# Third score chunk of the first token tile: from the attention heads to behind the last output projection

## The chip, the cores and the metric

The kernel runs on one core of a Trainium2 chip. The metric is the device time of one execution in microseconds (us). TensorE is called PE below, VectorE DVE, ScalarE ACT, GpSimd POOL, and SyncE SP; SP issues most of the loads from device memory. Each engine executes its own instructions in a fixed order and waits on semaphores for what others make. A "slot" is one buffer of a pool of on-chip memory: a load into a slot can start only when the last reader of what the slot held before is done.

## What is computed

One decoder layer on 512 tokens with 1024 features. Its first half is attention by two groups of heads, whose outputs are concatenated and projected (`w_o`). Its second half finds, for every token and each of 8 retrieval heads, 16 of 16384 experts by two sets of 128 keys:

```python
qp = (h @ w_pq).reshape(b, s, PEER_HEADS, 2, PEER_HALF)          # 1024 -> 2048 query features
sc = einsum("bshpd,hpnd->bshpn", qp, sub_keys)                   # 128 scores for each of 16 key sets
s1, i1 = top_k(sc[..., 0, :], 16);  s2, i2 = top_k(sc[..., 1, :], 16)
cand = s1[..., :, None] + s2[..., None, :]                       # pairs, then the best 16 of them
top_s, top_c = top_k(cand, 16);  gate = softmax(top_s)
# out = sum over the chosen experts e of gate_e * v_e * gelu(u_e . h)
```

`w_pq` is handled in four chunks of 512 columns (2 MB each). A chunk c gives the scores of two retrieval heads, that is four sets of 128 scores for each token.

## The kernel before

The 512 tokens are four tiles of 128. Tile 0 is the "sparse" tile: the rows of its chosen experts are gathered from memory. Tiles 1 to 3 are the "dense" ones: every expert is computed for them, in 128 blocks, and multiplied by a matrix of gates.

The program text gives an order of steps; a scheduler then sorts each engine's instructions by its own model. The stages, with their place in the profile before:

- Until about 206 us the modulation (`w_ada` through a pool called `g8` of two slots of 8 KB per partition, loaded as 1 MB pieces), then the input projections, then the heads of attention, tile 0 first and then tiles 3, 2, 1, to about 357 us.
- Into the heads of tiles 3, 2 and 1 a second list of steps is woven, `first`: for tile 0 its output projection, its second norm (`hidden2`), and for chunks 0, 1 and 2 the projection to queries and scores (`queries_one`, called `q1(c)`) followed by `top(0, c)`, the 16 best of each of the four score sets on DVE. A `q1` is 32 matmuls, recorded as 64, on L173, a copy `qpT` on ACT (L681), four matmuls against the keys (L685) and a copy `sc` on ACT (L687). `top(i, c)` calls `best`: two rounds of "8 largest" and "their places" for each set (L731 to L735).
- From 357 to 391 us the output projection of tiles 3, 2 and 1 (L385 to L387, three products of split numbers for every one). Then `hidden2` of these tiles, a norm, eight PE transposes (L136), a scale and shift (L167 on ACT, L165 on DVE), and a split into `h2hi` (ACT, L724) and `h2lo` (DVE, L725). Chunk 3 of tile 0, `q1(3)`, stands here.
- From 411 to 490 us `queries(T, c)` for the dense tiles together, four chunks, each with split weights `whi` (a cast on ACT, L373) and `wlo` (a subtraction on DVE, L374), woven with `top` of the chunk before.
- From about 490 us the dense pass in two halves: u (block inputs `ut`, split into `uhi` on ACT, L871, and `ulo` on DVE, L872; matmuls L940 to L942) to about 1050 us, and v (L986) to the end at 1684.5 us. Beside the first blocks runs the list `work`: `pick(0)`, which joins tile 0's best and chooses 16 experts per head in two halves of four heads (`select`, L743 to L778), then the remaining `top` steps, `pick` and `gates` of the dense tiles. The gathers of tile 0 follow its `pick`.

Where weights lie decides when they can be loaded. `w_pq` for `q1` goes through the pool `ld` of four slots of 4 KB per partition, so a chunk fills all four; `w_o` and the split weights of `queries` (L371, in `halves`) pass through the same four slots. `wload` doubles the piece when the pool is `g8`, and ties such a load behind the last load issued before it, by `issue_after`. The pool `g8` is free between the modulation and the score buffers `sc` of `queries`.

Of the kernel before, what the change touches and what calls it, by code (L numbers as in the profile page):

```python
# [38 lines left out]
DENSE = [1, 2, 3]  # L39
# [23 lines left out]
def pipe(tasks, lag=1):  # L63

    live, tasks, n = [], iter(tasks), 0
    while True:
        t = next(tasks, None)
        if t is not None:
            live.append((n, t))
        elif not live:  # L70
            return
        for s, g in reversed(live):
            if (n - s) % lag == 0 and next(g, live) is live:
                live = [x for x in live if x[1] is not g]
        n += 1
        yield


class Layer:
# [275 lines left out]
            self.wt[name] = self.wload(self.I[name], alloc)  # L355
        return self.wt[name]

    def weights1(self, name, src):

        if (name, 1) not in self.wt:  # L360
            self.wt[name, 1] = self.wload(src, self.ld)
        return self.wt[name, 1]

    def halves(self, name, src, raw, new):
# [271 lines left out]

    def w_pq1(self, c):
        self.keys("keys1", c)
        return self.weights1(f"w_pq{c}", self.I["w_pq"][c])

    def keys(self, name, c):

# [362 lines left out]
    def build(self):  # L1005
# [13 lines left out]
        def run(g):  # L1019
            for _ in g:  # L1020
                pass

        def seq(*gs):
            for g in gs:
                yield from g

        def weave(main, fill, n, skip=0, every=1, rest=True):
            for m, _ in enumerate(main):
                if m >= skip and (m - skip) % every == 0:
                    for _ in range(n):  # L1030
                        next(fill, None)
            if rest:
                run(fill)

        def spread(g, n):
            for _ in g:
                for _ in range(n):
                    yield

        def top(i, c):  # L1040
            self.best(i, T[i], c)
            yield

        def prep(f, *a):
            f(*a)
            yield

        def idle(n):
            for _ in range(n):
                yield  # L1050
# [18 lines left out]
        for g in (m[0], h0, h1, m[1], m[0], m[2], m[1], m[3], m[2], m[3], h0, h1):  # L1069
# [4 lines left out]
        q1 = lambda c: self.queries_one(T[0], c)  # L1074
        first = seq(prep(self.w_o, 0, 0), idle(1), self.out_proj(0, T[0], 0), prep(self.w_o, 0, 1), idle(1),
                    self.out_proj(0, T[0], 1), prep(self.w_pq1, 0), idle(2), spread(self.hidden2(0, T[0]), 3), idle(3),
                    spread(q1(0), 2), prep(self.w_pq1, 1), top(0, 0), spread(q1(1), 2), prep(self.w_pq1, 2), top(0, 1),
                    spread(q1(2), 2), top(0, 2))
        tasks = hs[2:] + base + self.heads(0, T)
        skip = len(tasks) + 10  # L1080
        main = pipe(tasks + self.heads(3, T) + self.heads(2, T) + self.heads(1, T), 3)
# [6 lines left out]
        run(first)  # L1088
        o = [self.out_proj(i, T[i], half) for i, half in ((3, 0), (2, 0), (1, 0), (3, 1), (2, 1), (1, 1))]
        n = [self.hidden2(i, T[i]) for i in (3, 2, 1)]  # L1090
        run(pipe(o[:3] + [prep(self.w_pq, 0)] + o[3:5] + n[:1] + o[5:] + [prep(self.w_pq1, 3)] + n[1:] + [q1(3)], 2))
        for c in range(4):
            tops = [top(i, c - 1) for i in DENSE if 0 < c < 3] + ([top(0, 3)] if c == 1 else [])
            weave(self.queries(T, c), seq(*tops), 1)
        work = seq(pick(0), *(top(i, c) for c in (2, 3) for i in DENSE),
                   *(g for i in DENSE for g in (pick(i), gates(i))))
# [64 lines left out]
```

## Time and profile before

| what | value |
|---|---|
| median of 3 runs | 1683.05 us (1680.65 to 1687.23) |
| profiled execution | 1686.27 us |
| its span on the core | 1684.5 us |
| granted PE clock, mean | 0.979 |
| PE busy | 1586.5 us, 94% of the span |
| DVE busy | 1261.8 us, 75% |
| ACT busy | 679.3 us, 40% |
| DMA | 451.36 MB, 268 GB/s |

A share of the whole span says little about the change, since it touches three stretches: the heads (to 357 us), the passage from the output projection to the first query products (391 to 435 us), and the sorting that runs on DVE from 434 us into the first dense blocks. Each is read for itself: which engine is full there, and what the others wait for. In the list of windows a row holds the bounds of a stretch, its length, then for PE, PE's weight loads, DVE, ACT and POOL the busy time with the count of instructions, the granted PE clock (1.00 is 2.4 GHz, 0.50 is 1.2 GHz), the DMA share and GB/s.

### The profile page before, as it was taken

To read this page: it belongs to the slowest core of one execution; us is meant where nothing else is said; L and a number is where in the kernel's file an instruction comes from. 1 tells how busy PE (TensorE), PEld (TensorE's weight loads), DVE (VectorE), ACT (ScalarE), POOL (GpSimd) and SP (SyncE) were. 2 spreads that over 40 slices of the span, in tenths; PEclk is the share of its full clock that TensorE was granted. 3 is DMA by queue.
4 is the path that set the end of the run, shared out by engine and by line. 5 is a ranking of instruction groups with operands and counts; after the bars stand their busy time and mean duration, and the time that the engine had idled before them with its cause. 6 is when DMAs were issued, how large, how long until landed. Compare 5 with 4: busy or idle time off the path is not lost.

```text
span 1684.5 us, 25155 instructions
## 1 busy us (share of the span) xinstructions
PE 1586.5 (94%) x8993; PEld 1392.5 (83%) x8993; DVE 1261.8 (75%) x2626; ACT 679.3 (40%) x1072; POOL 483.4 (29%) x514
## 2 busy tenths in 40 slices
PE   5999999998978999999999999999999999999996
PEld 2977498987977998999999999887777777877885
DVE  2533363586799789999998996687887788887863
ACT  3521364454323434663564465333333333333331
POOL 1302510001012455336226422223332323333311
PEclk7899999998989999999999999999999999999998
DMA  7354613358144788998999899999999999999852
GB/s 289 130 184 161 221 39 119 126 192 287 53 154 142 225 279 266 316 353 302 315 346 336 285 344 352 370 366 355 356 364 345 359 352 360 366 377 375 276 184 100
DMA packets 200913, 451.36 MB, mean 268 GB/s; under 512 B 17874, under 2 KB 103890, under 8 KB 198740
## 3 DMA queue, kind: packets, MB, share of 16 engines
q1 hardware_dynamic: 103252, 277.18, 46.4%
q0 software_dynamic: 38656, 139.48, 23.4%
q10 hardware_dynamic: 58880, 33.11, 6.5%
q8 instruction: 70, 1.15, 0.3%
q14 instruction: 55, 0.45, 0.1%
HBM read 393.07 MB, written 56.63 MB: 267 GB/s over the span
## 4 chain that ended last, share of the span: by engine, by line
PE 77%; DVE 10%; DMA 5%; ACT 3%; issue 2%; POOL 0%; SPq 0%; POOLq 0%; ACTq 0%; DVEq 0%
PE acc L986 30%; PE bank L942 7%; PE bank L941 7%; PE bank L940 7%; PE bank L386 4%; PE bank L387 4%; PE bank L173 4%; PE bank L385 4%; DVE ulo L872 3%; PE bank L820 2%; PE bank L136 2%; DMA G<-gst 2%; PE bank L564 2%; PE bank L579 2%; DMA ut<-in_peer_uT 1%
## 5 line engine op out<-in xcount | busy, mean ns | idle before, releaser
L986 PE MATMUL acc<-vhi,whl 128*128 128x512 f32 x1536 | 422.3, 393 | 22.7 <-ACT vhi L871 22.7
L986 PEld LDWEIGHTS acc<-vhi,whl 128*128 128x128 f32 x1536 | 287.3, 188 | 91.4 <-ACT vhi L871 29.2
L942 PE MATMUL bank<-hhi,ulo 128*128 128x384 f32 x1024 | 347.1, 339 | 15.4 <-DVE ulo L872 15.3
L940 PE MATMUL bank<-hhi,uhi 128*128 128x384 f32 x1024 | 345.5, 338 | 12.5 <-ACT uhi L871 12.4
L941 PE MATMUL bank<-hlo,uhi 128*128 128x384 f32 x1024 | 347.9, 340 | 0.0
L831 POOL DMA_INDIRECT gat<-in_peer_v,ids x128 | 155.6, 1216 | 325.7 <-DVE y L859 304.9
L871 ACT CAST uhi<-ut 128x1024 fp32r<-128x1024 f32 x128 | 134.4, 1050 | 275.5 <-PE bank L941 222.8
L831 POOL DMA_INDIRECT gat<-in_peer_u,ids x128 | 142.9, 1116 | 342.7 <-DVE sact L849 326.2
L986 PE MATMUL acc<-vlo,whl 128*128 128x512 f32 x768 | 239.2, 392 | 0.0
L872 DVE TENSOR_TENSOR ulo<-ut,uhi 128x1024 fp32r<-128x1024 f32 x128 | 170.7, 1334 | 58.1 <-ACT uhi L871 57.7
L942 PEld LDWEIGHTS bank<-hhi,ulo 128*128 128x128 f32 x1024 | 194.2, 190 | 21.1 <-DVE ulo L872 20.5
L940 PEld LDWEIGHTS bank<-hhi,uhi 128*128 128x128 f32 x1024 | 194.1, 190 | 14.6 <-ACT uhi L871 14.1
L941 PEld LDWEIGHTS bank<-hlo,uhi 128*128 128x128 f32 x1024 | 194.1, 190 | 0.5
L872 DVE TENSOR_TENSOR vlo<-vt,vhi 128x1024 fp32r<-128x1024 f32 x128 | 156.5, 1222 | 48.1 <-ACT vhi L871 46.4
L976 ACT CAST whl<-ge 128x384 fp32r<-128x384 f32 x128 | 65.4, 513 | 297.1 <-PE acc L986 279.6
L849 DVE CUSTOM_DVE_ANT_0 scr<-gat,h2r 128x1024 bf16<-128x1024 f32 x128 | 170.8, 1334 | 0.0
L986 PEld LDWEIGHTS acc<-vlo,whl 128*128 128x128 f32 x768 | 144.4, 188 | 31.9
L859 DVE SCALAR_TENSOR_TENSOR y<-gat,swgt,y 128x1024 f32<-128x1024 f32 x127 | 170.7, 1344 | 0.1
L871 ACT CAST vhi<-vt 128x1024 fp32r<-128x1024 f32 x128 | 133.7, 1048 | 79.5 <-PE acc L986 59.4
L977 DVE TENSOR_TENSOR whl<-ge,whl 128x384 fp32r<-128x384 f32 x128 | 71.0, 556 | 65.1 <-ACT whl L976 58.0
L822 ACT ACTIVATE gst<-bank 128x512 f32<-128x512 f32 x96 | 96.9, 1120 | 6.3 <-DMA G<-gst 6.3
L772 POOL TENSOR_TENSOR prod<-hit,cid 128x800 f32<-128x800 f16 x32 | 70.6, 2207 | 20.6 <-DVE hit L769 18.4
(252 smaller groups left out, 2231.6 us busy)
## 6 DMA issues: line engine op xcount, KB each, us to landing
ut<-in_peer_uT SPq DMA_DIRECT2D x128, 512.0 KB
vt<-in_peer_v SPq DMA_DIRECT2D x128, 512.0 KB
G<-gst ACTq DMA_DIRECT2D x24, 1024.0 KB
gt<-G SPq DMA_DIRECT2D x96, 256.0 KB
ged<-ge SPq DMA_DIRECT2D x120, 192.0 KB
ge<-ged SPq DMA_DIRECT2D x120, 192.0 KB
w<-in_w_ada SPq DMA_DIRECT2D x16, 1024.0 KB
w<-in_w_pq SPq DMA_DIRECT2D x32, 512.0 KB
```

The costliest lines, as they stand in the source:

```text
L772: g.tensor_tensor(out=prod, in0=hit, in1=cid[:, r][:, None, :, None].to_broadcast(shape), op=OP.mult)
L822: nc.scalar.activation(st[:, :, q + t4:q + t4 + 4].rearrange("p i t -> p t i"), pb.rearrange("p (t i) -> p t i", t=4), AF.Copy, scale=1.0 ...
L831: self.nc.gpsimd.indirect_dma_start(out=t, out_offset=None, in_=self.I[table], in_offset=bass.IndirectOffsetOnAxis(ap=ids[:, k:k + 1], axi ...
L849: v.tensor_tensor_reduce(out=scr, in0=u, in1=self.rows, op0=OP.mult, op1=OP.add, scale=1.0, scalar=0.0, accum_out=a[:, k:k + 1])
L859: v.scalar_tensor_tensor(out=self.y, in0=t, scalar=w[:, k:k + 1], in1=self.y, op0=OP.mult, op1=OP.add)
L871: nc.scalar.copy(hi, src)
L872: self.last_split = eng.tensor_tensor(out=lo, in0=src, in1=hi, op=OP.subtract)
L940: pe.matmul(A, uh[:, k, :], hh, start=(k == 0), stop=False)
L941: pe.matmul(A, uh[:, k, :], hl, start=False, stop=False)
L942: pe.matmul(A, ul[:, k, :], hh, start=False, stop=(k == KD - 1))
L977: nc.vector.tensor_tensor(out=wl, in0=w, in1=wh, op=OP.subtract)
L986: self.nc.tensor.matmul(self.acc[t][half], w[:, ts], v[:, half * 512:(half + 1) * 512], start=(b == n == 0), stop=(b == NK - 1 and n == 2))
```

## The change

`q1(2)` and `top(0, 2)` leave the list `first`. The weights of chunk 2 go into the two slots of `g8`, as two loads of 1 MB, and `q1(2)` stands behind the last output projection, ahead of `q1(3)`. Of the two steps that now sort after the heads, `top(0, 2)` is woven into the second chunk of `queries` and `top(0, 3)` into the third; before, `top(0, 3)` was in the second.

```diff
-    def weights1(self, name, src):
+    def weights1(self, name, src, alloc=None):
         if (name, 1) not in self.wt:
-            self.wt[name, 1] = self.wload(src, self.ld)
+            self.wt[name, 1] = self.wload(src, alloc or self.ld)
...
-        return self.weights1(f"w_pq{c}", self.I["w_pq"][c])
+        return self.weights1(f"w_pq{c}", self.I["w_pq"][c], self.g8 if c == 2 else self.ld)
...
-                    spread(q1(0), 2), prep(self.w_pq1, 1), top(0, 0), spread(q1(1), 2), prep(self.w_pq1, 2), top(0, 1),
-                    spread(q1(2), 2), top(0, 2))
+                    spread(q1(0), 2), prep(self.w_pq1, 1), top(0, 0), spread(q1(1), 2), top(0, 1))
...
-        run(pipe(o[:3] + [prep(self.w_pq, 0)] + o[3:5] + n[:1] + o[5:] + [prep(self.w_pq1, 3)] + n[1:] + [q1(3)], 2))
+        run(pipe(o[:3] + [prep(self.w_pq, 0)] + o[3:5] + n[:1] + o[5:]
+                 + [prep(self.w_pq1, 2), prep(self.w_pq1, 3)] + n[1:] + [q1(2), q1(3)], 2))
...
-            tops = [top(i, c - 1) for i in DENSE if 0 < c < 3] + ([top(0, 3)] if c == 1 else [])
+            tops = [top(i, c - 1) for i in DENSE if 0 < c < 3] + ([top(0, c + 1)] if c in (1, 2) else [])
```

On PE, behind the output projection, the transposes of tiles 2 and 1 (`xn`) and the projections of tile 0 (`x_2352`, its second-norm output) stand in this order, as a difference between the two programs:

```order
 L136 MATMUL bank<-ident,xn 128x128 x8
 L173 MATMUL bank<-x_2352,w 128x128 x32
-L136 MATMUL bank<-ident,xn 128x128 x16
-L685 MATMUL bank<-keys,qpT 128x128 x4
+L136 MATMUL bank<-ident,xn 128x128 x8
+L173 MATMUL bank<-x_2352,w 128x128 x32
+L136 MATMUL bank<-ident,xn 128x128 x8
+L685 MATMUL bank<-keys,qpT 128x128 x8
 L385 MATMUL bank<-h2hi,whi 128x384 x4
```

`q1(2)` takes the place that `q1(3)` had, and `q1(3)` stands between the transposes of tile 2 and those of tile 1, whose result every first product of the dense queries needs.

On ACT, from the copy of the queries of tile 0's last chunk on, before (`x_3405` is tile 2, `x_3435` tile 1, `whi` the split weights of the dense queries' chunk 1, `x` the scaled norm):

```order
L681 COPY qpT<-bank 128x512
L373 CAST whi<-w 128x1024
L167 ACTIVATE x_3405<-bank,b_119,a_118 128x128
L373 CAST whi<-w 128x1024
L167 ACTIVATE x_3405<-bank,b_119,a_118 128x128
L373 CAST whi<-w 128x1024
L167 ACTIVATE x_3435<-bank,b_119,a_118 128x128
L167 ACTIVATE x_3405<-bank,b_119,a_118 128x128
L724 CAST h2hi<-x_3405 128x2x128
```

and now (`x_3359` is tile 1; tile 2 is done ahead of this copy):

```order
L681 COPY qpT<-bank 128x512
L167 ACTIVATE x_3359<-bank,b_119,a_118 128x128 x2
L373 CAST whi<-w 128x1024
L167 ACTIVATE x_3359<-bank,b_119,a_118 128x128
L724 CAST h2hi<-x_3359 128x2x128
L687 COPY sc<-bank 128x512
L167 ACTIVATE x_3359<-bank,b_119,a_118 128x128
L724 CAST h2hi<-x_3359 128x2x128
L687 COPY sc<-bank 128x512
L373 CAST whi<-w 128x1024
```

One cast of chunk 1's weights still stands ahead of tile 1's first `h2hi`, and three stood ahead of tile 2's before; the two score copies of tile 0 stand between tile 1's `h2hi` casts.

On SP, the loads of weights, as a difference (L291 is `q1`'s, L371 that of split weights; 128x2048 is a piece in `g8`):

```order
 L371 DMA w<-in_w_pq 128x1024 x3
 L371 DMA w<-in_w_o 128x1024 x4
+L291 DMA w<-in_w_pq 128x2048 x2
 L291 DMA w<-in_w_pq 128x1024 x4
 L371 DMA w<-in_w_pq 128x1024 x12
```

Chunk 2's two pieces stand directly ahead of chunk 3's four; earlier in the list, four pieces of 0.5 MB for chunk 2 are gone.

On DVE the 16 instructions of "8 largest" and places that belong to `top(0, 2)`, with the four replacements between the rounds, leave the heads. The last steps of `select` for tile 0's first half now stand between the first `wlo` subtractions of `w_o`. By the order, the sorting instructions of `top(0, 2)` fall ahead of the ninth to thirteenth `ulo`; from the thirteenth `ulo` on, as many sorting instructions have passed as before.

## Rows read from the trace of the kernel before

**Rows 1.** Windows view: bounds, length, busy us (count) by engine, clock, DMA share, GB/s:

```profile
327.70:356.90 29.20, 28.67 (x255) 28.01 (x253) 27.43 (x169) 15.64 (x45) 2.87 (x12) 1.00 0.30 103
...
391.20:410.80 19.60, 12.79 (x98) 12.14 (x96) 12.86 (x24) 13.80 (x29) 4.45 (x8) 0.88 0.88 300
410.80:434.60 23.80, 23.61 (x129) 23.10 (x130) 12.55 (x34) 10.53 (x18) 0.00 (x0) 0.89 0.74 232
434.60:496.40 61.80, 56.62 (x353) 56.42 (x351) 59.43 (x378) 14.60 (x28) 7.22 (x21) 0.99 0.15 47
```

**Rows 2.** Chain that ended last, heads of attention: start us, us, what:

```profile
316.12 7.15 PE bank L173 x64
...
344.69 0.78 DVE tv L731 x4
...
357.13 1.14 DVE wlo L374
```

**Rows 3.** Timeline of PE: start us, us, line, operation, [idle before <-releaser]:

```profile
332.10 7.31 PE L173 MATMUL bank<-x,w 128*128 128x128 f32 x64
...
341.92 1.06 PE L685 MATMUL bank<-keys,qpT 128*128 128x128 f32 x8
...
392.10 7.31 PE L173 MATMUL bank<-x,w 128*128 128x128 f32 x64
401.49 1.09 PE L136 MATMUL bank<-ident,xn 128*128 128x128 f32 x8 [2.08 <-DVE xn L347]
...
404.72 1.69 PE L685 MATMUL bank<-keys,qpT 128*128 128x128 f32 x8
410.76 1.65 PE L385 MATMUL bank<-h2hi,whi 128*128 128x384 f32 x4 [4.35 <-ACT h2hi L724]
```

**Rows 4.** Timeline of DVE: a chunk of sorting, in the heads and later:

```profile
344.61 0.87 DVE L731 MAX8 tv<-sc 128x8 f32<-128x128 f32 x4
345.39 0.07 DVE L732 MATCH_VALUE_LOAD ti<-tv,sc 128x8 f32 x1
...
345.66 0.07 DVE L733 MATCH_VALUE_LOAD sc<-tv,sc 128x8 f32 x1
...
345.91 0.41 DVE L566 CUSTOM_DVE_ANT_0 s<-bank,mask 128x256 f32<-128x256 f32 x1
...
440.93 0.09 DVE L733 MATCH_VALUE_LOAD sc<-tv,sc 128x8 f32 x1
...
442.04 0.09 DVE L733 MATCH_VALUE_LOAD sc<-tv,sc 128x8 f32 x1
```

**Rows 5.** Timeline of SP's DMA issues of score weights:

```profile
375.42 7.39 SPq L291 DMA_DIRECT2D w<-in_w_pq  x4
398.10 32.84 SPq L371 DMA_DIRECT2D w<-in_w_pq  x12
```

**Rows 6.** Windows view, around the start of the dense queries (columns as before):

```profile
360.00:380.00 20.00, 19.96 (x89) 16.16 (x88) 14.76 (x17) 7.85 (x8) 0.00 (x0) 1.00 0.89 308
...
404.00:406.00 2.00, 2.00 (x12) 2.00 (x11) 2.00 (x3) 1.85 (x4) 0.62 (x2) 0.50 1.05 420
...
410.00:416.00 6.00, 5.05 (x15) 4.54 (x16) 6.00 (x26) 3.48 (x9) 0.00 (x0) 0.50 1.05 380
```

**Rows 7.** Timeline of ACT: first weight cast for the second query chunk:

```profile
402.73 1.05 ACT L373 CAST whi<-w 128x1024 fp32r<-128x1024 f32 x1 [1.51 <-DMA w<-in_w_pq]
```

**Rows 8.** Timeline of PE, queries at full clock:

```profile
418.89 0.33 PE L385 MATMUL bank<-h2hi,whi 128*128 128x384 f32 x1
419.06 0.33 PE L386 MATMUL bank<-h2lo,whi 128*128 128x384 f32 x1
```

**Rows 9.** Windows view, first blocks of the dense pass:

```profile
550.00:560.00 10.00, 9.06 (x53) 8.74 (x52) 6.63 (x29) 5.80 (x7) 6.59 (x7) 1.00 0.92 315
560.00:570.00 10.00, 10.00 (x59) 10.00 (x58) 6.75 (x8) 4.04 (x6) 5.24 (x3) 1.00 0.78 266
```

**Rows 10.** PE's waits, 440 to 1060 us: total, times, longest:

```profile
PE bank L942 <- DVE ulo L872: 15.3, 13, 3.4
```

## The prediction, made before the changed kernel ran

> **What bounds the kernel now.** I read the list of windows first, one row for each stretch that the change touches, then the chain of work that ended last, then the timelines of PE, DVE, ACT and SP inside these stretches. In the last 29.2 us of the heads PE is busy for 28.67 us and DVE for 27.43 [rows 1]: the two are nearly full together, ACT with 15.64 us is not. The chain runs there through DVE, from the end of one projection on PE to the first `wlo` of the output projection at 357.13 us [rows 2], so DVE's order of softmax pieces and sorting sets the end of the heads, and PE's fill is close behind it. Between the last output and the queries, 391.2 to 410.8 us, nothing is full: PE works 12.79 of 19.6 us [rows 1], and its timeline has two holes, one until 401.49 us, where the transposes wait for a norm, and one of 4.35 us until 410.76 us, where the first product waits for `h2hi` from ACT [rows 3]. From 410.8 to 434.6 us PE is full (23.61 of 23.8) and DVE half idle; from 434.6 to 496.4 us DVE is full (59.43 of 61.8) [rows 1]. Work that leaves the heads therefore leaves a full stretch, and its PE part goes to a loose one, its DVE part to one that is as full as the one it left.
>
> **The heads: less of both engines.** On PE `q1(2)` is one block of 7.31 us and four key products, 1.06 us recorded for eight interleaved records, about half of it new time [rows 3]: 7.31 + 0.53 = 7.8 us go, and 28.67 - 7.8 = 20.9 us stay. On DVE the price of a chunk of sorting is read from start to next start, because the recorded times overlap: the four first "8 largest" take 345.39 - 344.61 = 0.78 us, a first search with its load 345.66 - 345.39 = 0.27, a replacement with its load 345.91 - 345.66 = 0.25 [rows 4]. With 0.2 for a single "8 largest", the chunk is 0.78 + 4 x 0.27 + 4 x (0.25 + 0.2 + 0.27) = 4.7 us. About 1.3 us of the last `select` steps leave as well (eight short instructions of 0.1 to 0.2 us, estimated from the same rows). DVE keeps 27.43 - 4.7 - 1.3 = 21.4 us. If DVE's idle time in the stretch (29.2 - 27.43 = 1.8) stays, the stretch takes 23.2 us, 6.0 less. With no idle time it is 21.4, 7.8 less. At the other end, a heads stage that waits on its own softmax chain, from scores to DVE to ACT to PE, keeps half of it: 3.0 less. I take **-6.0**, nearest to the engine that the chain names.
>
> **The output projection.** The `select` steps of 1.3 us now stand between the first four `wlo`. PE's first products there wait for these. Some of the steps fall before the first product anyway, so I take **+0.3**, from 0 to +1.3.
>
> **From the last output to the queries.** `q1(2)` fits where `q1(3)` was, 392.10 to 399.4 us (times of before, without the shift). Tile 2's transposes keep 401.49 to 402.4 us, since their norm is not earlier. `q1(3)` then takes 7.31 us at full clock, to 409.8; but the granted clock was 0.50 (1.2 GHz) at 404 to 406 us, after the hole in PE's work before 401.49 [rows 3, 6], and if the block runs so until 406 us, 1.8 us are added: 409.8 to 411.6, I take 410.7. Only as it ends are the four `ld` slots free, so the loads of the dense queries' chunk 1 are issued at about 410.7 instead of 398.10 [rows 5]. Their first cast had its data 402.73 - 398.10 = 4.6 us after the issue [rows 5, 7], beside other transfers; at the 308 GB/s of 360 to 380 us [rows 6], a load of 0.5 MB alone would be 1.7 us. On ACT this cast now stands ahead of tile 1's first `h2hi`. Cast, scale and split cost 1.05 us [rows 7] and, by the 0.4 us of a small copy here, about 0.8 more. The first product then starts at 410.7 + (1.7 to 4.6) + 1.8 = 414.2 to 417.1; I take 415.6, 4.8 later than before. That is not all lost, because those products ran at a granted clock of 0.50 until 416 us [rows 6]: the first thirty took 418.89 - 410.76 = 8.1 us [rows 3, 8], and at 0.17 us each [rows 8] take 5.2. If PE has its full clock, since it worked on `q1(3)` through what was a hole, they end at 420.8 against 418.9: **+1.9**. Ends: 414.2 at full clock gives +0.5, 417.1 at half clock +6.3.
>
> This is where a rule speaks. In this trace the clock was 0.50 after each of the two holes, and the new order closes part of the second hole and leaves one of some 3 to 4 us behind the transposes of tile 1. The Trainium skill (TensorE: Matmul & The Clock Gate, Part 1) says that the throttled state is the default and that activity releases it. Read for the new order, it grants the full clock behind 9 us of projection work, and the term is +1.9; the row at 410 us, where a hole of 4.35 us was followed by 1.2 GHz, would make it 415.6 + 8.1 - 418.9 = +4.8, and the whole sum +0.1.
>
> **Loads on SP.** 2 MB stand ahead of chunk 3's weights, on the way from 375.42 us [rows 5]; at 308 GB/s [rows 6] they delay these by 6.8 us. But `q1(3)` reads them at 402.4 instead of 392.1, 10.3 us later. **0**; without this cover, in case the two `g8` pieces start only with the last load issued before them, up to +3.
>
> **The sorting on DVE.** The 4.7 us of `top(0, 2)` now lie behind 434 us. Done alone, its rounds are dependent steps of 442.04 - 440.93 = 1.11 us [rows 4] instead of 0.72, so up to 6.3 us. By the order it passes ahead of the ninth to thirteenth `ulo`, and PE waits for `ulo` 15.3 us in 13 waits [rows 10], so a late `ulo` is paid. But DVE was busy for only 6.63 and 6.75 us of the two stretches of 10 us from 550 us [rows 9], where the twelfth and later `ulo` fall: 3.4 + 3.2 us can take it up. I take **+1.0**, nearest to these rows; ends 0 and +4.7. What follows on all engines differs by swaps of neighbours in the order only; 0, from -3 to +3.
>
> **Sum.** -6.0 + 0.3 + 1.9 + 0 + 1.0 = -2.8 us. The profiled execution took 1686.27 us, so by it 1683.5; the median of the runs is 3.2 us lower, and I predict for it: 1683.05 - 2.8 = 1680.2, **1680 us**. Differences under 0.5%, 8.4 us, are about what cannot be told from no change here.
>
> **Rivals.**
>
> A. The full PE block counts: the heads shrink by 7.8 us, the loads land early, the DVE work is all taken up. -7.8 + 0.3 + 0.5 + 0 = -7.0: 1676 us. For it: both engines lose that much in a full stretch. Against it: DVE's chain has small waits that PE's block does not make.
>
> B. Slower, by ACT's order. The weight cast ahead of tile 1's `h2hi` holds the dense queries: `q1(3)` ends at 411.6, the load lands 4.6 us later, the first product starts at 418.0, and PE, idle since the transposes, gets 1.2 GHz as at 410 to 416 us. 418.0 + 8.1 - 418.9 = +7.2; with -6.0 + 0.3 + 1.0 the sum is +2.5: 1685.5 us. It decides from a first product at 415.5 us at half clock, or 418.4 at full clock, on (+4.7 over the 418.9 of before). For it: the cast waited for this very load before. Against it: that load came beside others at a DMA share over 1.
>
> C. The block of `q1(2)` was hidden: the softmax chain sets the heads' end and gives back only 3.0 us. -3.0 + 0.3 + 1.9 + 1.0 = +0.2: 1683 us. For it: the chain holds the block of `q1(1)` at 316.12 us [rows 2], and DVE's work where `q1(2)` ran. Against it: DVE was full, and loses 6 us.
>
> **How the numbers follow.** The forecast has 0.45 (its own range, with half of the bounds, 1677 to 1684), A 0.15, B 0.25, C 0.15. The unknown swaps of -3 to +3, the DVE bound (+3.7 over what I take) on top of B, and -3 below A widen the range to 1673 to 1690. Below 1674.6, faster by over 0.5%: A with a gain from the swaps, 0.14. Above 1691.5: B with the sorting paid in full and adverse swaps, 0.14. Within: 0.72.
>
> **What would show it.** The profile after should have the first `wlo` of `w_o` about 6 us earlier, at 351 us, with DVE over nine tenths busy before it; a block L173 of 7 to 9 us directly behind tile 2's transposes; the wait of the first product L385 still for `h2hi`, with ACT's cast L373 waiting for its load just before; PE at 1.00 in the first products; and sorting of 128 scores on DVE behind 434 us, with fewer idle us at 550 to 570 on the old scale. The heads ending less than 3 us earlier, or the first dense query product more than 5 us later in relation to the last output than before, would prove the sum wrong, as would a difference that arises only beyond 570 us.

## The result and the profile after

The changed kernel took 1674.27 us (median; the kernel before 1683.83 in the runs beside it), a ratio of 0.9947 with a 95% interval of 0.9934 to 0.9960, which is 8.9 us faster (the medians differ by 9.6). One of its six runs, at 1702.64 us with a lower granted clock, is left out of the ratio. A second set of rounds gave 0.9957 (0.9942 to 0.9972), 7.2 us. The forecast was 1680 us, 2.8 less than before, in a range of 1673 to 1690. The direction and the range held; the size was three times the sum.

The profiled execution took 1674.09 us with a span of 1672.1, 12.4 less than the span before. 2.25 us of that lie before 297 us, in a part that the change does not touch: DVE, ACT and POOL run the same instructions in the same order up to there in both programs, and a second trace of the unchanged kernel reached the same point 1.47 us earlier than the first did. So everything below is counted from the start of `q1(1)`, from landmark to landmark. Each kernel has two traces; the numbers are their lengths in us, each read from the starts of the two instructions named.

| stretch, from start to start | before | after | difference of means |
|---|---|---|---|
| heads: `q1(1)` to the first product of `w_o` (L385) | 40.92, 40.92 | 32.71, 32.71 | -8.2 |
| output projection: to the first transpose behind it (L136) | 34.36, 34.35 | 34.19, 34.21 | -0.2 |
| passage: to the key products of the first dense queries (L666) | 39.10, 38.95 | 43.61, 43.82 | +4.7 |
| sorting: to the 18th `ulo` | 152.07, 151.89 | 151.57, 151.19 | -0.6 |
| u half: to block 120 | 485.67, 484.62 | 485.26, 485.96 | +0.5 |
| v half: block 120 to block 150 | 128.10, 128.09 | 127.68, 127.67 | -0.4 |
| v half: block 150 to block 180 | 135.36, 135.35 | 130.79, 131.08 | -4.4 |
| block 180 to the end | 352.97, 351.75 | 352.59, 351.43 | -0.4 |

Blocks are counted by `ulo` and `vlo` subtractions on DVE, from 0. The differences sum to -9.0 us, about the measured gain. Three rows carry it: the heads, the passage, and thirty blocks in the v half, 800 us behind the change.

The windows after that answer to [rows 1] (the bounds moved with the work; columns as there):

```profile
325.45:346.40 20.95, 20.69 (x182) 19.93 (x181) 20.33 (x127) 14.07 (x42) 1.72 (x9) 1.00 0.09 34
380.60:406.34 25.74, 20.70 (x170) 20.32 (x168) 10.38 (x23) 11.80 (x28) 4.56 (x9) 0.93 0.62 197
406.34:428.50 22.16, 21.90 (x129) 20.99 (x130) 17.34 (x47) 13.71 (x21) 0.00 (x0) 1.00 0.89 299
428.50:490.00 61.50, 57.29 (x353) 56.70 (x352) 58.63 (x340) 14.56 (x26) 5.97 (x17) 0.98 0.17 57
```

The last stretch of the heads that took 29.20 us takes 20.95, and both engines are still full in it (20.69 and 20.33 us). From the first transpose to the first product the granted clock is 0.93 instead of 0.88, and 1.00 in the stretch behind it, where it was 0.89. DVE has 17.34 us of work in that stretch instead of 12.55; sorting that was thought to lie further on is 2.2 us more, `wlo` subtractions are 4.3 us more, other steps are less.

PE's timeline after, for [rows 3]:

```profile
346.41 0.71 PE L385 MATMUL bank<-whi,oTh 128*128 128x512 f32 x2
...
380.60 1.03 PE L136 MATMUL bank<-ident,xn 128*128 128x128 f32 x8
381.47 7.31 PE L173 MATMUL bank<-x,w 128*128 128x128 f32 x64
391.89 1.97 PE L136 MATMUL bank<-ident,xn 128*128 128x128 f32 x8 [3.12 <-DVE xn L347]
393.65 8.10 PE L173 MATMUL bank<-x,w 128*128 128x128 f32 x64
401.59 1.04 PE L136 MATMUL bank<-ident,xn 128*128 128x128 f32 x8
...
406.34 1.37 PE L385 MATMUL bank<-h2hi,whi 128*128 128x384 f32 x4 [1.93 <-ACT h2hi L724]
...
424.21 2.17 PE L666 MATMUL bank<-keys,qpT 128*128 128x128 f32 x18
```

The order is the one that the section on the change shows: `q1(2)` at 381.47 where `q1(3)` was, tile 2's transposes, `q1(3)` at 393.65 in 8.10 us, tile 1's transposes only at 401.59. The first product of the dense queries starts at 406.34 us, 25.74 us behind the first transpose (380.60) instead of 19.53. Its wait for `h2hi` is 1.93 us, and was 4.35. Over the whole passage, from the first transpose to the key products, PE's account is, before and after (columns as in [rows 1]):

```profile
391.23:430.33 39.10, 32.10 (x194) 30.98 (x192) 22.79 (x55) 22.28 (x42) 4.45 (x8) 0.87 0.85 276
380.60:424.21 43.61, 38.30 (x265) 37.01 (x264) 25.09 (x67) 23.44 (x44) 4.56 (x9) 0.96 0.76 247
```

PE is busy for 6.2 us more and idle for 1.7 us less (7.00 before, 5.31 after). Its mean clock went from 0.87 to 0.96, and so its busy time rose by less than the 8 us that the added block and its keys take.

The chain that ended last, after, from the start of the output projection to the first sorting of dense scores (start, us, what):

```profile
346.43 1.14 DVE wlo L374
...
376.57 5.12 DMA xd<-x
...
391.89 1.97 PE bank L136 x8
393.86 6.56 PE bank L173 x52
400.44 4.12 DMA w<-in_w_pq
404.59 1.04 ACT whi L373
...
428.51 0.86 DVE tv L731 x4
```

Two transfers stand in it. New is `xd`, the store of tile 3's sum, behind which ACT may overwrite `x`. The other is the load of the second weight chunk, issued at 400.44 us, 1.3 us ahead of the end of `q1(3)`, for which the cast at 404.59 waits ahead of tile 1's `h2hi`. That load stood in the chain before as well:

```profile
398.55 5.71 DMA w<-in_w_pq
404.28 1.05 ACT whi L373
```

In the v half, the window of blocks 150 to 180, and PE's only notable wait in it, first before and then after:

```profile
1196.17:1331.53 135.36, 126.08 (x543) 101.28 (x542) 110.00 (x150) 44.16 (x61) 41.37 (x38) 1.00 0.97 351
```

```profile
PE acc L986 <- ACT vhi L871: 9.3, 6, 1.5
```

```profile
1188.72:1319.51 130.79, 125.95 (x545) 101.75 (x544) 110.04 (x151) 45.08 (x62) 39.18 (x38) 1.00 0.99 369
```

```profile
PE acc L986 <- ACT vhi L871: 4.6, 3, 1.5
```

PE has the same work in both (126.08 and 125.95 us). It waits six times for `vhi` before and three times after, 1.55 us each, and the window is 4.6 us shorter.

### The profile page after: what moved, and what is told of

Same layout as the page of the kernel before. It is cut to its first block, busy times and chain, and to the rows that moved or that the text cites. A ratio compares the mean times of both kernels' runs of the same rounds, so it can differ in the third digit from the quotient of the medians.

```text
span 1672.1 us, 25156 instructions
## 1 busy us (share of the span) xinstructions
PE 1584.6 (95%) x8993; PEld 1390.0 (83%) x8993; DVE 1262.7 (76%) x2626; ACT 679.5 (41%) x1072; POOL 487.3 (29%) x514
## 4 chain that ended last, share of the span: by engine, by line
PE 75%; DVE 14%; DMA 3%; ACT 2%; issue 2%; POOL 1%; ACTq 0%; POOLq 0%; DVEq 0%; SPq 0%
PE acc L986 29%; PE bank L942 8%; PE bank L941 8%; PE bank L940 8%; PE bank L173 4%; PE bank L820 3%; PE bank L386 3%; DVE ulo L872 3%; PE bank L387 2%; PE bank L385 2%; PE bank L136 2%; PE bank L564 2%; PE bank L579 2%; DVE scr L849 1%; DVE ti L735 1%
## 5 line engine op out<-in xcount | busy, mean ns | idle before, releaser
L831 POOL DMA_INDIRECT gat<-in_peer_v,ids x128 | 161.6, 1263 | 328.7 <-DVE y L859 309.1
```

Source lines behind the costliest of these rows:

```text
L831: self.nc.gpsimd.indirect_dma_start(out=t, out_offset=None, in_=self.I[table], in_offset=bass.IndirectOffsetOnAxis(ap=ids[:, k:k + 1], axi ...
```

## The experiments

**The two kernels again.** No edit; a second trace of each.

> The kernel before, unchanged, for a second trace. The first pair of traces differs by 2.25 us in the first 210 us, where the change has no part, and by about 5 us between 1060 us and the end. Theory 'chance': this trace reaches the first output-projection product 356.87 us minus 0 to 3 us in, and the time from the last ulo of the u half (120th, 1068 us) to the end comes out 3 to 6 us shorter than the 616 us of the first trace. Theory 'real': the stretch behind 1060 us stays within 1.5 us of its first length in both kernels, and the changed kernel keeps some 5 us less there. Ratio to the kernel before 1.000 +- 0.001 in both.

> The changed kernel, unchanged, for a second trace and more rounds. Ratio to the kernel before 0.9947 +- 0.0015. From the start of q1(1) to the first output-projection product 32.7 us (before: 40.9), from there to the first transpose behind it 34.2 in both, from there to the key products of the first dense queries 43.6 us (before: 39.1): these three should repeat within 0.5 us. Theory 'chance' gives a stretch behind 1060 us that differs by over 1.5 us from the 611 us of the first trace of the changed kernel; theory 'real' repeats it.

Ratios 1.0007 (0.9993 to 1.0021) and 0.9957 (0.9942 to 0.9972). The table above holds both traces. Every stretch repeats within 0.5 us except the long ones from the 18th `ulo` to block 120 and from block 180 to the end, which move by 0.7 to 1.2. The 135.4 and 130.9 us in the v half repeat within 0.3, so "chance" falls: this gain belongs to the changed program, though the change has nothing there. The time before 297 us is chance: it differs by 1.5 us between two traces of one program.

**Where the v half's gain comes from.** The scheduler sorts instructions by its own model of time, and the order that it finds in the v half is not the same in the two programs. On DVE the listings of before and after are alike ahead of block 145 or so, part there, and are alike again from about block 178 on but for some swaps behind block 224: most of the rows that differ are those of the thirty blocks whose time differs. They begin so (`y` and `sact` are tile 0's gathered experts, `whl` and `ge` the gates; the reads of accumulators are left out):

```
before                                after
ge<-ge,gt                             ge<-ge,gt
whl<-ge,whl                           ge<-ge,gt
ge<-ge,gt                             ge<-ge,gt
vlo<-vt,vhi                           vlo<-vt,vhi
scr,sact<-gat,h2r                     scr,sact<-gat,h2r
ge<-ge,gt                             whl<-ge,whl
whl<-ge,whl                           vlo<-vt,vhi
```

All kernels that were run can be sorted by DVE's order in these blocks, since each was scheduled anew:

| DVE's order in blocks 145 to 178 | kernels | blocks 150 to 180, us |
|---|---|---|
| that of before (in the second to fourth with two other rows at its edge) | before twice; swapped slots; `q1(3)` in the queries; both edits; chunk 3 last | 135.36, 135.35; 135.40; 135.41; 135.36; 135.40 |
| that of after | after twice; early load | 130.79, 131.08; 130.63 |
| three others, each its own | sorting alone; `q1(2)` twice; chunk 3 behind | 132.08; 132.06; 132.09 |

The same order has the same length within 0.5 us, whatever the heads and the passage did. (From block 150 on the first and the third kernel of the last row have one order on DVE.) ACT's order changes together with DVE's, and the traces name it as what PE waits for. The first of PE's waits before, on ACT and then on PE:

```profile
1198.85 0.51 ACT L976 CAST whl<-ge 128x384 fp32r<-128x384 f32 x1 [2.71 <-PE acc L986]
1202.96 0.51 ACT L976 CAST whl<-ge 128x384 fp32r<-128x384 f32 x1 [3.60 <-PE acc L986]
1203.38 1.04 ACT L871 CAST vhi<-vt 128x1024 fp32r<-128x1024 f32 x1
```

```profile
1204.47 1.66 PE L986 MATMUL acc<-vhi,whl 128*128 128x512 f32 x6 [1.55 <-ACT vhi L871]
```

Two casts `whl` stand in a row ahead of the cast `vhi` here. The second of them waits 3.60 us for PE's products; only then does ACT make the `vhi` that PE needs next, and PE stands still for the two casts. Each further `vhi` is as late until two of them follow each other again. Such waits are six in every trace of the first row of the table, three in the second, four in the third, and the length less 1.55 us for each is 125.9 to 126.4 us in all twelve. So the place of a few casts on ACT accounts for the 4.4 us. No run moved one cast alone.

**The sorting alone**, in the kernel before:

```diff
-                    spread(q1(2), 2), top(0, 2))
+                    spread(q1(2), 2))
...
-([top(0, 3)] if c == 1 else [])
+([top(0, c + 1)] if c in (1, 2) else [])
```

> The kernel before with one part of the change alone: q1(2) stays in the heads and its weights in the ordinary slots, only top(0,2) moves to the dense queries. Theory 'both engines are full' (the heads shrank by 8.2 us because PE lost 7.8 us and DVE 6.0 us): with PE's block kept, the heads shrink by 0 to 1.5 us only, ratio 0.999 to 1.001. Rival 'DVE sets the heads' (the chain names DVE): the heads shrink by 4 to 6 us, ratio 0.997.

Ratio 0.9993 (0.9979 to 1.0007). The heads took 39.78 us, 1.1 less. The passage took 41.22 us, 2.2 more than before, with the same work for PE: it was idle for 8.3 us instead of 7.0, at a clock of 0.83 instead of 0.87. The output projection was 1.3 us longer and the u half 3.2; blocks 150 to 180 were 3.3 shorter.

**`q1(2)` twice**, in the kernel before:

```diff
+        if c == 2:
+            for j in range(4):
+                js = slice(j * P, (j + 1) * P)
+                self.mm(pb[:, js], lambda k: w(k)[:, js], lambda k: T["h2"][:, k, :], KD)
```

> The kernel before with the 32 matmuls of q1(2) done twice in the heads, the first result overwritten by the second: 7.3 us more of PE there, nothing more for DVE. Theory 'PE sets the heads' (PE was busy 28.67 of 29.2 us, and moving the sorting alone did nothing): from the start of q1(1) to the first output-projection product 47 to 48.5 us instead of 40.9, ratio 1.004 to 1.005. Rival 'DVE sets the heads' (the chain of waits names DVE): 40.9 to 43 us, ratio under 1.0015.

The heads took 47.42 us, 6.5 more, of 7.15 us of added matmuls. The ratio was only 1.0017 (1.0001 to 1.0032): the program was given another order in the v half (132.06 us), and that pays back 3.3. Four windows from the start of `q1(1)` to the first product of `w_o` settle what sets the heads: before, after, sorting alone, PE twice.

```profile
315.95:356.87 40.92, 40.39 (x359) 39.73 (x358) 32.68 (x193) 20.39 (x59) 2.87 (x12) 1.00 0.34 116
```

```profile
313.70:346.41 32.71, 32.45 (x288) 31.68 (x286) 25.61 (x151) 18.88 (x56) 1.72 (x9) 1.00 0.21 72
```

```profile
313.72:353.50 39.78, 39.64 (x354) 39.16 (x353) 30.38 (x173) 19.79 (x59) 2.86 (x12) 1.00 0.34 118
```

```profile
314.41:361.83 47.42, 46.88 (x419) 46.43 (x418) 32.75 (x192) 20.11 (x59) 2.85 (x12) 1.00 0.29 100
```

PE is idle for 0.53, 0.26, 0.14 and 0.54 us. DVE goes from 32.68 to 25.61, 30.38 and 32.75, and the length does not follow it: taking 2.3 us of DVE's work away shortens the stretch by 1.1, adding 6.5 us of PE's lengthens it by 6.5. PE sets the heads.

**Chunk 3 in the modulation's slots** instead of chunk 2, in the changed kernel:

```diff
-self.g8 if c == 2 else self.ld)
+self.g8 if c == 3 else self.ld)
```

> The changed kernel with chunk 3 in the modulation's slots and chunk 2 in the ordinary ones, so that the ordinary slots come free with q1(2), one projection earlier, and the loads of the dense queries' second weight chunk are issued about 8 us earlier. Theory 'late load' (the passage lost 4.5 us because ACT's weight cast stands ahead of tile 1's h2hi and waits for a load issued at 400.4): the first product of the dense queries starts 2 to 4 us earlier against the last output, the passage from the last output to the key products falls from 43.6 to 39.5 to 41.5 us, ratio to before 0.992 to 0.9935. Rival 'more work in the passage' (q1(3), transposes and keys fill PE and ACT): no change, 0.9947. Rival 'DMA crowding' (the loads run beside the hd stores and delay these): passage longer by 1 us or more.

Slower: ratio 1.0023 (1.0007 to 1.0039), passage 48.21 us. The loads of the second weight chunk were issued earlier, at 389.47 us, so the part of the edit that was meant took place. ACT's and PE's timelines show what went against it:

```profile
386.03 0.46 ACT L167 ACTIVATE x<-bank,b,a 128x128 f32<-128x128 f32 x1 [6.36 <-DMA xd<-x]
...
408.38 0.59 ACT L681 COPY qpT<-bank 128x512 f32<-128x512 f32 x1 [3.67 <-DMA hd<-h2lo]
```

```profile
396.18 1.97 PE L136 MATMUL bank<-ident,xn 128*128 128x128 f32 x8 [5.88 <-DVE xn L347]
...
411.80 1.56 PE L385 MATMUL bank<-h2hi,whi 128*128 128x384 f32 x4 [1.62 <-ACT h2hi L724]
```

ACT waits 6.36 us for the store `xd` (3.65 in the changed kernel), and tile 2's transposes wait 5.88 us for the norm behind it: they start 14.06 us behind the first transpose instead of 11.3. That is 2.7 of the 4.5 us that the passage is longer, and the wait for `xd` ends at 386.03 us, before 389.47, so the earlier loads did not cause it; why the store took longer was not isolated. Behind them ACT waits 3.67 us for a store `hd` (the split hidden state, written to memory), 2.2 in the changed kernel, which is what "DMA crowding" foretold. "Late load" is not tested cleanly by this run. Beside that the v half kept the order of before, and the u half was 8 us longer, though every engine has the order of the other runs in blocks 20 to 120; this was not followed up. The traced execution was the slowest of this version's eight (1698.35 us, median 1690.23).

**An early load**: chunk 2's two pieces in the heads, in the changed kernel:

```diff
-spread(q1(1), 2), top(0, 1))
+spread(q1(1), 2), prep(self.w_pq1, 2), top(0, 1))
...
-                 + [prep(self.w_pq1, 2), prep(self.w_pq1, 3)]
+                 + [prep(self.w_pq1, 3)]
```

> The changed kernel with chunk 2's two 1 MB loads issued in the heads, right behind the weights of chunk 1, instead of beside the output projection. Theory 'crowded stores' (the 2 MB stand in the DMA engines ahead of tile 3's store xd, for which ACT waits 3.65 us before it may overwrite x; in the kernel before it did not wait): that wait goes, tile 2's transposes start 10.3 us after the first transpose behind the output projection instead of 11.3, the passage to the key products of the first dense queries falls from 43.7 to about 42.7 us, ratio to before 0.9940 to 0.9955. Rival 'order alone': the passage stays at 43.6 to 43.8.

Ratio 0.9964 (0.9946 to 0.9983), passage 43.37 us, against 43.6 and 43.8. The wait for the store did go; on ACT in its place stands one for PE:

```profile
383.94 0.89 ACT L167 ACTIVATE x<-bank,b,a 128x128 f32<-128x128 f32 x2 [3.53 <-PE bank L136]
```

The output projection became 1.4 us longer (35.59). So the 3.65 us that ACT waited for `xd` cost the passage only some 0.2 to 0.5 us: the theory "crowded stores" names a wait, not the loss.

**`q1(3)` in the first dense queries**, in the changed kernel:

```diff
-n[1:] + [q1(2), q1(3)], 2))
+n[1:] + [q1(2)], 2))
...
-weave(self.queries(T, c), seq(*tops), 1)
+weave(self.queries(T, c), seq(*([q1(3)] if c == 0 else tops)), 1)
```

> The changed kernel with q1(3) woven into the first dense queries instead of ahead of them; the weight casts of the dense queries' second chunk then stand on ACT behind tile 1's h2hi. Theory 'late load' (tile 1's h2hi waits for q1(3) on PE and for a cast on ACT whose load waits for q1(3)'s slots): the first product starts 16 to 20 us after the first transpose instead of 25.8, and since q1(3) now stands among the products, the key products follow at 40.5 to 42.5 us instead of 43.7; ratio to before 0.993 to 0.995. Rival 'PE is what fills the passage' (the same matmuls in another order): 43.5 us or more.

Slower: 1.0015 (1.0001 to 1.0029). The first product came 21.27 us behind the first transpose instead of 25.8, nearly as "late load" had it, and yet the key products came at 48.12 instead of 43.7. An earlier first product gained nothing, since PE then did `q1(3)` among the products, and the holes ahead of it stayed empty: PE was idle for 8.7 us of this passage, 5.3 in the changed kernel. The v half had the order of before (135.41).

**Both edits**, the early load and `q1(3)` in the queries:

> Both edits together: chunk 2's weights loaded in the heads, and q1(3) woven into the first dense queries. If both theories hold, their gains add: key products 39.5 to 41.5 us after the first transpose, ratio to before 0.9925 to 0.9945, the fastest of all. If the passage is only PE work, 43.5 us as in the changed kernel.

Ratio 1.0037 (1.0018 to 1.0057), passage 47.20 us. Neither theory's gain is there.

**Chunk 3 moved on as well**, in the changed kernel, into the last dense queries:

```diff
-                 + [prep(self.w_pq1, 2), prep(self.w_pq1, 3)] + n[1:] + [q1(2), q1(3)], 2))
+                 + [prep(self.w_pq1, 2)] + n[1:] + [q1(2)], 2))
...
-([top(0, c + 1)] if c in (1, 2) else [])
+([top(0, 2)] if c == 1 else [])
+            tops += [prep(self.w_pq1, 3), q1(3), top(0, 3)] if c == 3 else []
```

> The changed kernel with chunk 3 moved on as well: its weights load behind those of the last dense queries, q1(3) and top(0,3) stand woven into these. Theory 'the passage is PE work' (behind 391 us PE had 7 us of holes and a clock of 1.2 GHz for some 9 us; q1(2) uses the same hole that q1(3) used, and q1(3) on top of it fills what is left and 4.6 us more): with q1(2) alone the passage to the key products takes 39 to 40.5 us as in the kernel before, and the block of 7.3 us goes where DVE is full: 152 to 155 us from the key products to the eighteenth ulo. The order of DVE's instructions in the v half is that of the kernel before, so 135.4 us from block 150 to block 180, against 130.8 in the changed kernel. Total from the start of q1(1) 1357 to 1361 us, ratio to before 0.994 to 0.996. Rival 'the block only moves' (PE is full there too): 159 us to the eighteenth ulo, ratio 0.997 or more.

Ratio 1.0033 (1.0018 to 1.0048). The passage was 41.58 us with one projection in it, 2.0 to 2.2 shorter than with two and 2.6 longer than before; the stretch to the 18th `ulo` was 162.72, 11.3 longer than after. PE in 61 us from the key products on, here and in the changed kernel:

```profile
420.70:482.00 61.30, 61.30 (x404) 61.30 (x403) 48.65 (x253) 13.86 (x26) 0.53 (x1) 1.00 0.19 59
```

```profile
424.20:485.00 60.80, 60.80 (x386) 60.71 (x384) 56.26 (x309) 14.35 (x27) 4.40 (x9) 1.00 0.13 40
```

PE is full in both, and DVE is not (48.65 and 56.26 us). The rival "the block only moves" was right in kind: the stretch that was read as DVE's has no room on PE. The 11.3 us are 3.7 more than it foretold (159 us), and that was not traced.

**The same, behind the queries**: the steps of chunk 3 in the list behind the four chunks.

```diff
+        run(seq(prep(self.w_pq1, 3), q1(3), top(0, 3)))
```

> As the run with chunk 3 in the last dense queries, but with its steps in the list behind them. On DVE the order in the last third of the v half is that of the changed kernel, as in the run that moved the sorting alone. Theory 'the v half goes by the order of instructions, whatever happened before': 131 to 132.5 us from block 150 to block 180 here, 135.4 in the other run, and a ratio lower by 0.002 for that alone (0.992 to 0.994). Rival 'the v half goes by when it starts': both runs give the same length there.

Ratio 1.0009 (0.9993 to 1.0024), 3.3 us less in blocks 150 to 180 than the run before it (132.09 against 135.40), the length that was expected from the order, but for a reason only half right: the listing agrees with that of after behind block 178, and is one of its own ahead of it. That the length goes by the order and not by the start is what the two runs show. 165.11 us to the 18th `ulo`: the place is as poor as the last. None of these versions beats the changed kernel.

## Why the prediction was right in direction and short in size

**The heads, -6.0 forecast, -8.2 measured.** This step is the first that was mis-sized. The chain of waits passes through DVE there [rows 2], and I let DVE's 21.4 us and its idle time set the new length. PE had 0.53 us of idle time in the whole stretch from `q1(1)` on, DVE 8.2 (40.92 - 32.68). The window of 29.2 us [rows 1] began where DVE was full and hid that. PE's loss was the term, as rival A had it: in the two windows above its busy time fell by 7.9 us (40.39 to 32.45) and its idle time by 0.3. The forecast's 7.8 counted the key products with half of their recorded time. Rival C, the hidden block, is refuted by the doubled block.

**The output projection, +0.3 forecast, -0.2 measured.** The `select` steps between the first `wlo` cost nothing.

**The passage, +1.9 forecast, +4.7 measured.** The mechanism was there, mis-sized in two terms. `q1(3)` took 8.10 us, as reckoned with part of it at 1.2 GHz; the load came 4.15 us after its issue (400.44 to 404.59), near the upper end of my range, and the first product was 6.3 us later against the output projection, not 4.8. The clock was 1.00 behind it, so the products to the key products took 17.87 us (406.34 to 424.21) instead of 19.57, 1.7 less and not 2.9: the first thirty took 6.4 us at full clock, where I had counted 5.2 without their waits for `h2hi` and `h2lo`. The Trainium skill (TensorE: Matmul & The Clock Gate, Part 1) has activity release the throttled state; the trace agrees, with 1.00 from 406.34 us on after the block `q1(3)`, where 0.50 stood before [rows 6]. What I missed is the account of PE's time: of a second block of 7.3 us and its keys, only 1.7 us fall into holes that were there. The runs that took `q1(3)` out show it from the other side, and only in part: with one block the passage took 41.4 and 41.6 us, 2.0 to 2.4 less than with two, and not the 39.0 of the kernel before. The run that moved the sorting alone had one block as well and took 41.2, 2.2 more than before. So some 2 to 2.5 of the 4.7 us go with the second block, and the rest with the move of `top(0, 2)` or the order that it brought, which the forecast left out here; by which wait it costs them is open. In rival B the first product was to be 7.2 us later and at half clock as well; it was nearly as late, the half clock did not come. In the run with chunk 3 in the last dense queries the 2.5 us over the kernel before are idle time of PE (9.4 us, 7.0 before), and waits of ACT for `hd` stores stand there.

**Loads on SP, 0 forecast.** `q1(3)` did not wait for its weights. But they met a store that I did not look at: ACT waited 3.65 us for `xd`, and did not when these loads came early. By that run it cost 0.2 to 0.5 us.

**The sorting, +1.0 forecast, -0.6 measured.** The place was read wrongly in part. In front of the dense scores DVE now does the first rounds of both chunks of tile 0, eight first maxima and eight searches, where it did four of each before; so some 2 us of the 4.7 never reach the stretch behind 434 us. That stretch took up the rest: from 485 us to the 18th `ulo` DVE worked 83.7 of 90.8 us, and 80.4 of 92.4 from 490 us on before. The room was there, as [rows 9] had promised.

**The order behind, 0 forecast with -3 to +3, -4.4 in thirty blocks of the v half alone.** This is the step that failed. I counted swaps of neighbours as nothing, and two orders of the same instructions differ by 4.4 us there: a cast `whl` ahead of a cast `vhi` on ACT makes PE wait 1.55 us, three times more before than after. With the other stretches behind the 18th `ulo` the sum is -4.7, outside of the -3 to +3.

So 8.9 us are 8.2 from PE in the heads, less 4.7 in the passage, 4.4 by a new order far behind, and 1.0 of small terms. The forecast's direction rested on the heads, rightly; a sum of 4.4 us, half of the net gain, comes from an order that nobody chose. That is luck, and so is part of the rest: the four stretches up to the 18th `ulo` gave -4.3 us against the -2.8 forecast, with two terms off by 2.2 and 2.8 us in opposite directions. Two of the signs that the prediction had named against its own sum came, a first product more than 5 us later and a difference beyond 570 us.

## What to carry to other kernels

Where two engines look full, take the longest stretch that ends at the same landmark and subtract: the one with half a microsecond of idle time sets the length, and the chain of waits may still name the other. A block moved into a passage with holes costs what the holes don't hold, so account for PE's whole time there, not for the first wait; and what else the edit moves has a price there as well. And where a scheduler sorts the whole program, an edit can deal a new order far away from it: compare traces by stretches from landmark to landmark, and judge a version by the sum only after the stretches that the edit cannot reach are known.

## What the runs showed that was not expected

A stretch of the same program repeats within 0.4 us in most places, even 40 us of three busy engines (40.92 and 40.92, 32.71 and 32.71), while the first 300 us differ by 1.5 us between two traces of one program. And one program text with one projection moved can differ by 4.4 us in thirty blocks that hold the same instructions in another order, because three more casts come too late for PE.
